# A two-layer hybrid decoder trunk: a joined last product, an enforced order of the wide matmuls, and the weight tiles below the residual tiles

## The chip, the cores and the metric

The kernel runs on one core of one Trainium2 chip. The metric is the device time of one execution in microseconds, the median of several runs. The core has TensorE (matmuls into PSUM), VectorE (DVE in the profile), ScalarE (ACT), GpSimd (POOL), a queue SP that issues most transfers, and 16 DMA engines. SBUF is the working memory on 128 partitions; PSUM has eight banks of 128 x 512 fp32.

## The reference

A causal decoder trunk on 256 tokens of width 2048, in fp32, with two layers. Cut to what matters:

```python
for l in range(2):
    h = rmsnorm(x, norm_mix[l])
    x = x + (even_mixer if l == 0 else odd_mixer)(h, ...)   # in-projection, mixing, out-projection
    h = rmsnorm(x, norm_ffn[l])
    x = x + conv_ffn(h, ffn_w_up[l], ffn_conv_w[l], ffn_w_down[l])
return rmsnorm(x, norm_final)

def conv_ffn(h, w_up, conv_w, w_down):
    g, u = split(h @ w_up)            # 2048 -> 2 x 5632
    g = causal_dwconv(g, conv_w)      # width 3, along the tokens
    return (silu(g) * u) @ w_down     # 5632 -> 2048
```

Layer 0 mixes with a dilated sliding-window attention beside a convolution module; layer 1 with a forgetting attention of 16 heads. Every weight is read once from HBM, about 410 MB in all, and every matmul is to keep nearly full fp32 accuracy.

## The kernel before, in words

**Split operands.** A weight or activation is held as hi + lo, two tiles of a reduced fp32 type that one matmul pass takes: hi is the rounded value, lo the rest. A product takes hi·hi, hi·lo and lo·hi.

**The weight stream.** `stream` (L79) loads 1 MB of weights per transfer into one of three `raw` buffers, and for each half ScalarE makes the hi tile (L95) and VectorE the lo tile (L96), with a raised priority (`AHEAD`). hi and lo have four buffers each in the pool `wp`. A new pair of tiles can be made once TensorE has finished with the pair four before.

**Wide products.** `panel_b` (L100) computes four 128-channel blocks of an output panel over all 256 tokens. The weights stand in the array; the moving operand is the split activation, hi and lo side by side. So for each weight tile there is one matmul of 512 columns with the hi weights (L111, `acc_g`, `acc_u`, `acc_d` and so on by the product's name) and one of 256 columns with the lo weights (L115). A panel over 16 k-tiles has 64 such pairs. The products g and u (up-projection, 22 panels each), d (down-projection of layer 0), q and k of layer 1, `oc` and `ob` (out-projections) run so; the moving operand is `xs` for g, u, q and k, the hidden tile `hp` for d, and `y2` for the out-projections. Layer 0's in-projections use the narrow form (`wide=False`, three matmuls of 256 columns). `panel_a` (L131) is the other way round: the activations stand, 512 weight columns move, three matmuls per k-tile (L127 to L129).

**What sets the order.** The program is traced in order, and a planner then orders each engine's instructions by priority and by the time at which it reckons their inputs ready. Within one engine that order is fixed when the program runs. So the matmuls of a wide product stand in the order the planner gave, which is not everywhere the traced one (hi, lo, hi, lo): where it reckons a lo tile late, it puts several hi matmuls ahead.

**Memory.** Pools are laid out in SBUF in the order in which they are opened: `keep` (constants, the residual stream `xT` and its split form `xs`), then `wp` (raw, hi, lo), then `wk` and what the layers open. In PSUM, `pacc` has five banks for the products' sums and `pms` three for the rest.

**The end.** Layer 1's FFN calls `down1` (L618) twice. The second call handles the last 20 k-tiles of the down-projection in token-major form (`acc_e`). It first closes the scope of both PSUM pools (L629) and opens one pool with eight banks, one for each of four output panels and two token halves. It then goes through the k-tiles four at a time for all panels, and the last four in two steps of two. In the last step all four panels are done for the first token half and then for the second, with `finish_rows` (L660) after each: it adds the residual (L616), sums squares on ScalarE (L664), takes the reciprocal root (`rsqrt_cols`, L154), multiplies by the norm's weights on GpSimd (L669), scales on VectorE and ScalarE (L673, L675), and issues one output transfer a panel (L676).

Of the kernel before, what the change touches and what calls it, by code (L numbers as in the profile page):

```python
# [37 lines left out]
AHEAD, BEHIND, TAIL = 400, 300, 60  # L38
# [3 lines left out]
def trunk(ctx, tc, a):  # L42
    nc = tc.nc
    V, S, PE, G = nc.vector, nc.scalar, nc.tensor, nc.gpsimd

# [53 lines left out]

    def panel_b(src_of, x2, kts, name, order=(0, 1, 2, 3), dk=4, wide=True):  # L100
# [3 lines left out]
        acc = {m: pacc.tile([P, 512], F32, tag="acc", name=f"acc_{name}_{m}") for m in order}  # L104
        for ks, hi, lo in stream(src_of, len(kts), P * len(order), name, dk):
            for m in order:
                ms = slice(m * P, (m + 1) * P)
                for j, k in enumerate(ks):
                    x = x2(kts[k])
                    if wide:  # L110
                        PE.matmul(acc[m], hi[:, j, ms], x.rearrange("p a t -> p (a t)"), start=k == 0, stop=False)  # L111
# [3 lines left out]
                    PE.matmul(acc[m][:, :T], lo[:, j, ms], x[:, 0, :], start=False, stop=k == len(kts) - 1)  # L115
# [38 lines left out]
    def rsqrt_cols(ps, scale, name, n=2):  # L154
# [7 lines left out]
        V.tensor_tensor(out=t, in0=r, in1=r, op=ALU.mult)  # L162
        V.tensor_tensor(out=t, in0=t, in1=v, op=ALU.mult)
# [496 lines left out]
    def finish_rows(acc, t):  # L660
        for i in range(4):
            cs = slice(512 * i, 512 * (i + 1))
            add_o(acc[i][t], t, i)
            S.activation(junk[:, 512 * (i % 2):512 * (i % 2) + 512], o[:, t, cs], AF.Square, accum_out=fs[:, t, i:i + 1])  # L664
        V.reduce_sum(out=sf[:, t:t + 1], in_=fs[:, t, :], axis=AX.X)
        rf = rsqrt_cols(sf[:, t:t + 1], 1.0 / D, f"fin{t}", 1)
        for i in range(4):
# [72 lines left out]
```

## Time and profile before

| | |
|---|---|
| runs | 2240.04, 2237.7, 2239.58 us; median 2239.58 |
| the profiled execution | 2240.73 us; its span 2238.9 us, granted TensorE clock 0.996 |
| TensorE (matmul) | busy 2213.6 us, 99% of the span |
| VectorE, ScalarE, GpSimd | 67%, 50%, 1% |
| HBM read | 409.84 MB, 184 GB/s over the span |

The span runs from the first to the last instruction; the execution's time is 1.8 us longer. Matmuls are pipelined: a row's duration is longer than the distance to the next matmul's start, so rates are read from start to start. In a row of the timeline stand start, duration, engine, source line, operation, output<-inputs, shapes and count, and in brackets the idle time before it and what released it. A row of windows has the stretch, its length, the busy time and count of each engine (TensorE's matmuls, its weight loads, VectorE, ScalarE, GpSimd), the granted clock, the DMA share and GB/s. A row of the groups has the count, then busy us, mean ns, idle before and its releasers.

### The profile page before, as it was taken

To read this page: it belongs to the slowest core of one execution; us is meant where nothing else is said; L and a number is where in the kernel's file an instruction comes from. 1 tells how busy PE (TensorE), PEld (TensorE's weight loads), DVE (VectorE), ACT (ScalarE), POOL (GpSimd) and SP (SyncE) were. 2 spreads that over 40 slices of the span, in tenths; PEclk is the share of its full clock that TensorE was granted. 3 is DMA by queue.
4 is the path that set the end of the run, shared out by engine and by line. 5 is a ranking of instruction groups with operands and counts; after the bars stand their busy time and mean duration, and the time that the engine had idled before them with its cause. 6 is when DMAs were issued, how large, how long until landed. Compare 5 with 4: busy or idle time off the path is not lost.

```text
span 2238.9 us, 31976 instructions
## 1 busy us (share of the span) xinstructions
PE 2213.6 (99%) x12778; PEld 1944.4 (87%) x12778; DVE 1493.3 (67%) x2280; ACT 1120.4 (50%) x1579; POOL 26.0 (1%) x58
## 2 busy tenths in 40 slices
PE   8999999999999999999999999999999999999997
PEld 8999988888888888888888888888888888888886
DVE  6999988767754577666655555677666644676644
ACT  6567665544443445444554554455544433454433
POOL 0000000000000000000000000000000000000001
PEclk9999999999999999999999999999999999999999
DMA  8544445555555555555544444555555555555453
GB/s 289 182 183 169 162 177 188 188 188 189 188 188 188 188 188 189 188 189 188 189 173 170 170 170 170 188 183 193 188 188 188 188 190 195 188 185 188 168 194 122
DMA packets 60806, 414.08 MB, mean 185 GB/s; under 512 B 7296, under 2 KB 8000, under 8 KB 12272
## 3 DMA queue, kind: packets, MB, share of 16 engines
q1 hardware_dynamic: 59904, 410.72, 51.2%
q8 instruction: 100, 1.64, 0.3%
q10 hardware_dynamic: 144, 1.05, 0.1%
q0 software_dynamic: 608, 0.26, 0.0%
q14 instruction: 50, 0.41, 0.0%
HBM read 409.84 MB, written 2.10 MB: 184 GB/s over the span
## 4 chain that ended last, share of the span: by engine, by line
PE 97%; DMA 1%; DVE 1%; ACT 0%; SPq 0%; issue 0%; ACTq 0%; DVEq 0%
PE acc_g L111 15%; PE acc_u L111 14%; PE acc_g L115 7%; PE acc_u L115 7%; PE acc_d L111 7%; PE acc_d L115 4%; PE acc_oc L111 3%; PE acc_k L111 3%; PE acc_q L111 3%; PE acc_q L115 2%; PE acc_k L115 2%; PE acc_d L127 2%; PE acc_d L129 2%; PE acc_v L128 2%; PE acc_v L129 2%; PE acc_v L127 2%
## 5 line engine op out<-in xcount | busy, mean ns | idle before, releaser
L111 PE MATMUL acc_g<-xs,whi_g 128*128 128x512 f32 x1408 | 493.0, 397 | 0.0
L111 PE MATMUL acc_u<-xs,whi_u 128*128 128x512 f32 x1408 | 481.9, 395 | 0.0
L115 PE MATMUL acc_g<-xs,wlo_g 128*128 128x256 f32 x1408 | 388.7, 280 | 0.0
L115 PE MATMUL acc_u<-xs,wlo_u 128*128 128x256 f32 x1408 | 370.0, 279 | 0.0
L96 DVE TENSOR_TENSOR wlo_g<-raw_g,whi_g 128x1024 fp32r<-128x1024 f32 x176 | 215.2, 1224 | 166.3 <-ACT whi_g L95 166.3
L111 PEld LDWEIGHTS acc_g<-xs,whi_g 128*128 128x128 f32 x1408 | 262.6, 188 | 60.5
L111 PEld LDWEIGHTS acc_u<-xs,whi_u 128*128 128x128 f32 x1408 | 260.1, 188 | 52.7
L95 ACT CAST whi_u<-raw_u 128x1024 fp32r<-128x1024 f32 x176 | 185.1, 1052 | 239.6 <-PE acc_u L111 122.0
L96 DVE TENSOR_TENSOR wlo_u<-raw_u,whi_u 128x1024 fp32r<-128x1024 f32 x176 | 213.3, 1222 | 116.2 <-ACT whi_u L95 116.2
L95 ACT CAST whi_g<-raw_g 128x1024 fp32r<-128x1024 f32 x176 | 184.9, 1052 | 198.3 <-PE acc_u L111 93.3
L96 DVE TENSOR_TENSOR wlo_d<-raw_d,whi_d 128x1024 fp32r<-128x1024 f32 x136 | 166.5, 1225 | 161.4 <-ACT whi_d L95 161.2
L115 PEld LDWEIGHTS acc_u<-xs,wlo_u 128*128 128x128 f32 x1408 | 265.0, 188 | 9.0
L115 PEld LDWEIGHTS acc_g<-xs,wlo_g 128*128 128x128 f32 x1408 | 265.6, 189 | 3.0 <-DVE wlo_g L96 0.2
L95 ACT CAST whi_d<-raw_d 128x1024 fp32r<-128x1024 f32 x136 | 143.0, 1051 | 207.2 <-PE acc_d L111 118.8
L111 PE MATMUL acc_d<-hp,whi_d 128*128 128x512 f32 x704 | 245.2, 394 | 0.0
L115 PE MATMUL acc_d<-hp,wlo_d 128*128 128x256 f32 x704 | 194.4, 283 | 0.0
L111 PEld LDWEIGHTS acc_d<-hp,whi_d 128*128 128x128 f32 x704 | 131.3, 188 | 28.8
L115 PEld LDWEIGHTS acc_d<-hp,wlo_d 128*128 128x128 f32 x704 | 132.4, 188 | 1.9
L115 PE MATMUL acc_q<-xs,wlo_q 128*128 128x256 f32 x384 | 106.0, 283 | 0.0
L115 PE MATMUL acc_k<-xs,wlo_k 128*128 128x256 f32 x384 | 105.8, 281 | 0.0
L111 PE MATMUL acc_q<-xs,whi_q 128*128 128x512 f32 x256 | 90.6, 396 | 0.0
L96 DVE TENSOR_TENSOR wlo_e<-raw_e,whi_e 128x1024 fp32r<-128x1024 f32 x40 | 48.9, 1225 | 60.4 <-ACT whi_e L95 60.4
(305 smaller groups left out, 4178.0 us busy)
## 6 DMA issues: line engine op xcount, KB each, us to landing
raw_g<-in_ffn_w_up SPq DMA_DIRECT2D x88, 1024.0 KB, 4.7
raw_u<-in_ffn_w_up SPq DMA_DIRECT2D x88, 1024.0 KB, 4.8
raw_d<-in_ffn_w_down SPq DMA_DIRECT2D x68, 1024.0 KB, 4.7
raw_q<-in_od_w_in SPq DMA_DIRECT2D x16, 1024.0 KB, 4.8
raw_k<-in_od_w_in SPq DMA_DIRECT2D x16, 1024.0 KB, 4.8
raw_v<-in_od_w_in SPq DMA_DIRECT2D x16, 1024.0 KB, 4.7
raw_oc<-in_od_w_out SPq DMA_DIRECT2D x16, 1024.0 KB, 4.8
raw_e<-in_ffn_w_down SPq DMA_DIRECT2D x16, 1024.0 KB, 4.8
```

The costliest lines, as they stand in the source:

```text
L95: S.copy(hi, rv[:, h:h + half, :])
L96: last = V.tensor_tensor(out=lo, in0=rv[:, h:h + half, :], in1=hi.bitcast(F32), op=ALU.subtract)
L111: PE.matmul(acc[m], hi[:, j, ms], x.rearrange("p a t -> p (a t)"), start=k == 0, stop=False)
L115: PE.matmul(acc[m][:, :T], lo[:, j, ms], x[:, 0, :], start=False, stop=k == len(kts) - 1)
L127: PE.matmul(o, xh, hi, start=first, stop=False)
L128: PE.matmul(o, xh, lo, start=False, stop=False)
L129: PE.matmul(o, xl, hi, start=False, stop=last)
```

## The change

It has five parts.

1. The pool `wp` is opened ahead of `keep`, so the weight tiles lie at lower addresses and `xT` and `xs` above them.
2. `in_order` adds, for every matmul of the wide products, a dependency on the one traced before it, with no semaphore: the planner must keep the traced order within and across wide products. Other matmuls can still stand between.
3. The last product keeps the PSUM pools: three of its eight sums take the banks of `pms` and five those of `pacc`.
4. The last four k-tiles of the last product are loaded in four transfers of 1 MB and split into eight pairs of tiles that all stay: two pairs in the tiles of the gate (`gp`, `cv`), one in a spare `hp` tile, four in the normal buffers, one in a `raw` buffer. Then for each token half, and in it for each panel, come 12 matmuls, the residual's add, the squares and, for panels 0 to 2, the multiplication with the norm's weights, now on VectorE. After the four panels come the reciprocal root and the scaling in the order 1, 0, 3, 2, which for panel 3 includes the norm's weights.
5. In `rsqrt_cols`, for one column, two multiplications become one instruction.

```diff
-    keep = ctx.enter_context(tc.tile_pool(name="keep", bufs=1))
     wp = ctx.enter_context(tc.tile_pool(name="wp", bufs=4))
+    keep = ctx.enter_context(tc.tile_pool(name="keep", bufs=1))
...
-                    hi = room.tile([P, half, width], F32R, tag="gp", name=f"whi_{name}_{c + h}", bufs=2)
-                    lo = room.tile([P, half, width], F32R, tag="cv", name=f"wlo_{name}_{c + h}", bufs=2)
+                    hi, lo = room(f"{name}_{c + h}")
...
+    issued = [None]
+
+    def in_order(*args, **kw):
+        i = PE.matmul(*args, **kw).ins
+        if issued[0] is not None:
+            tc.add_manual_dep(i, issued[0].name, mybir.DependencyInfo(mybir.DependencyClass.NoSync, mybir.DependencyReason.DATA),
+                              reason="order of a product's matmuls")
+        issued[0] = i
...
+        mm = in_order if wide else PE.matmul
...
-                        PE.matmul(acc[m], hi[:, j, ms], x.rearrange("p a t -> p (a t)"), start=k == 0, stop=False)
+                        mm(acc[m], hi[:, j, ms], x.rearrange("p a t -> p (a t)"), start=k == 0, stop=False)
...
-        V.tensor_tensor(out=t, in0=r, in1=r, op=ALU.mult)
-        V.tensor_tensor(out=t, in0=t, in1=v, op=ALU.mult)
+        if n == 1:
+            V.scalar_tensor_tensor(out=t, in0=r, scalar=v, in1=r, op0=ALU.mult, op1=ALU.mult)
...
-        ps_scope.close()
-        pl = ctx.enter_context(tc.tile_pool(name="pl", bufs=1, space=bass.MemoryType.PSUM))
-        acc = [[pl.tile([P, 512], F32, name=f"acc_e{i}{t}") for t in range(2)] for i in range(4)]
+        acc = [[None, None] for i in range(4)]
+        for b, (i, t) in enumerate((i, t) for i in range(4) for t in range(2)):
+            acc[i][t] = misc(f"acc_e{i}{t}") if b < 3 else pacc.tile([P, 512], F32, tag="acc", name=f"acc_e{i}{t}")
...
-        for i in range(4):
-            for got in part(i, at, KC):
-                for t in range(2):
-                    rows(i, t, at, *got)
-        at = n - KC
-        last = [next(part(i, at, KC, room=fp if i > 1 else None)) for i in range(4)]
+        rooms = [from_gate] * 2 + [from_hidden] + [from_weights] * 4 + [from_raw]
+        last = [list(part(i, at, 4, room=lambda nm: rooms.pop(0)(nm))) for i in range(4)]
         for t in range(2):
             for i in range(4):
-                rows(i, t, at, *last[i])
-            with tc.high_priority(offset=TAIL * t):
-                finish_rows(acc, t)
+                for got in last[i]:
+                    rows(i, t, at, *got)
+                add_o(acc[i][t], t, i)
+                cs = slice(512 * i, 512 * (i + 1))
+                S.activation(junk[:, 512 * (i % 2):512 * (i % 2) + 512], o[:, t, cs], AF.Square, accum_out=fs[:, t, i:i + 1])
+                if i < 3:
+                    V.tensor_tensor(out=o[:, t, cs], in0=o[:, t, cs], in1=gb[:, cs], op=ALU.mult)
+            V.reduce_sum(out=sf[:, t:t + 1], in_=fs[:, t, :], axis=AX.X)
+            rf = rsqrt_cols(sf[:, t:t + 1], 1.0 / D, f"fin{t}", 1)
+            for i in (1, 0, 3, 2):
+                cs = slice(512 * i, 512 * (i + 1))
+                if i == 3:
+                    V.scalar_tensor_tensor(out=o[:, t, cs], in0=o[:, t, cs], scalar=rf, in1=gb[:, cs], op0=ALU.mult, op1=ALU.mult)
+                elif i == 1:
+                    V.tensor_scalar(out=o[:, t, cs], in0=o[:, t, cs], scalar1=rf, scalar2=None, op0=ALU.mult)
+                else:
+                    S.activation(o[:, t, cs], o[:, t, cs], AF.Copy, scale=rf)
+                nc.sync.dma_start(out=a["out"][t * P:(t + 1) * P, cs], in_=o[:, t, cs])
```

`from_gate`, `from_hidden`, `from_weights` and `from_raw` each return a hi and a lo tile of two k-tiles by 512 columns from the tiles named in part 4; `from_hidden` and `from_raw` cut both out of one larger tile.

More of the change, by code (lines that the diff above doesn't have):

```diff
@@ L37 @@
 ACT_TAPS = (1,)
-AHEAD, BEHIND, TAIL = 400, 300, 60
+AHEAD, BEHIND = 400, 300
 @with_exitstack
@@ L44, in trunk @@
     V, S, PE, G = nc.vector, nc.scalar, nc.tensor, nc.gpsimd
+    wp = ctx.enter_context(tc.tile_pool(name="wp", bufs=4))
     keep = ctx.enter_context(tc.tile_pool(name="keep", bufs=1))
-    wp = ctx.enter_context(tc.tile_pool(name="wp", bufs=4))
     wk = ctx.enter_context(tc.tile_pool(name="wk", bufs=2))
-    ps_scope = ctx.enter_context(ExitStack())
-    pacc = ps_scope.enter_context(tc.tile_pool(name="pacc", bufs=5, space=bass.MemoryType.PSUM))
-    pms = ps_scope.enter_context(tc.tile_pool(name="pms", bufs=3, space=bass.MemoryType.PSUM))
+    pacc = ctx.enter_context(tc.tile_pool(name="pacc", bufs=5, space=bass.MemoryType.PSUM))
+    pms = ctx.enter_context(tc.tile_pool(name="pms", bufs=3, space=bass.MemoryType.PSUM))
     def misc(name):
@@ L110, in panel_b @@
                     if wide:
-                        PE.matmul(acc[m], hi[:, j, ms], x.rearrange("p a t -> p (a t)"), start=k == 0, stop=False)
+                        mm(acc[m], hi[:, j, ms], x.rearrange("p a t -> p (a t)"), start=k == 0, stop=False)
                     else:
-                        PE.matmul(acc[m][:, :T], hi[:, j, ms], x[:, 0, :], start=k == 0, stop=False)
-                        PE.matmul(acc[m][:, :T], hi[:, j, ms], x[:, 1, :], start=False, stop=False)
-                    PE.matmul(acc[m][:, :T], lo[:, j, ms], x[:, 0, :], start=False, stop=k == len(kts) - 1)
+                        mm(acc[m][:, :T], hi[:, j, ms], x[:, 0, :], start=k == 0, stop=False)
+                        mm(acc[m][:, :T], hi[:, j, ms], x[:, 1, :], start=False, stop=False)
+                    mm(acc[m][:, :T], lo[:, j, ms], x[:, 0, :], start=False, stop=k == len(kts) - 1)
         return acc
@@ L161, in rsqrt_cols @@
         t = wk.tile([P, n], F32, tag="rs_t", name=f"t_{name}")
-        V.tensor_tensor(out=t, in0=r, in1=r, op=ALU.mult)
-        V.tensor_tensor(out=t, in0=t, in1=v, op=ALU.mult)
+        if n == 1:
+            V.scalar_tensor_tensor(out=t, in0=r, scalar=v, in1=r, op0=ALU.mult, op1=ALU.mult)
+        else:
+            V.tensor_tensor(out=t, in0=r, in1=r, op=ALU.mult)
+            V.tensor_tensor(out=t, in0=t, in1=v, op=ALU.mult)
         V.tensor_scalar(out=t, in0=t, scalar1=-0.5, scalar2=1.5, op0=ALU.mult, op1=ALU.add)
@@ L646, in down1, with from_gate, from_hidden @@
                         rows(i, t, at, *got)
-        at = n - 4
-        for i in range(4):
-            for got in part(i, at, KC):
-                for t in range(2):
-                    rows(i, t, at, *got)
-        at = n - KC
-        last = [next(part(i, at, KC, room=fp if i > 1 else None)) for i in range(4)]
+        def from_gate(nm):
+            return [fp.tile([P, KC, 512], F32R, tag=tag, name=f"{w}_{nm}", bufs=2) for tag, w in (("gp", "whi"), ("cv", "wlo"))]
+        def from_hidden(nm):
+            both = fp.tile([P, 4, 2, T], F32R, tag="hp", name=f"wboth_{nm}", bufs=6).rearrange("p a b t -> p (a b t)")
+            return [both[:, 1024 * h:1024 * (h + 1)].rearrange("p (k c) -> p k c", k=KC) for h in range(2)]
@@ new lines, in from_weights, with from_raw @@
+        def from_weights(nm):
+            return [wp.tile([P, KC, 512], F32R, tag=w, name=f"{w}_{nm}") for w in ("whi", "wlo")]
+        def from_raw(nm):
+            both = wp.tile([P, 2 * KC * 512], F32, tag="raw", name=f"wboth_{nm}", bufs=3).bitcast(F32R)
+            return [both[:, 1024 * h:1024 * (h + 1)].rearrange("p (k c) -> p k c", k=KC) for h in range(2)]
+        rooms = [from_gate] * 2 + [from_hidden] + [from_weights] * 4 + [from_raw]
+        at = n - 4
+        last = [list(part(i, at, 4, room=lambda nm: rooms.pop(0)(nm))) for i in range(4)]
@@ L654, in down1 @@
         for t in range(2):
             for i in range(4):
-                rows(i, t, at, *last[i])
-            with tc.high_priority(offset=TAIL * t):
-                finish_rows(acc, t)
[L660 to L667, printed above, removed]
-            cs = slice(512 * i, 512 * (i + 1))
-            G.tensor_tensor(out=o[:, t, cs], in0=o[:, t, cs], in1=gb[:, cs], op=ALU.mult)
-        for i in range(4):
-            cs = slice(512 * i, 512 * (i + 1))
-            if i % 2 == 0:
-                V.tensor_scalar(out=o[:, t, cs], in0=o[:, t, cs], scalar1=rf, scalar2=None, op0=ALU.mult)
-            else:
-                S.activation(o[:, t, cs], o[:, t, cs], AF.Copy, scale=rf)
-            nc.sync.dma_start(out=a["out"][t * P:(t + 1) * P, cs], in_=o[:, t, cs])
+                for got in last[i]:
+                    rows(i, t, at, *got)
```

1 line of the change is left out of this document (added).

## The prediction

> **What bounds the kernel now.** I read the page first: engine totals, the chain that ended last, the costliest groups.
>
> ```profile
> span 2238.9 us, 31976 instructions
> ...
> PE 2213.6 (99%) x12778; PEld 1944.4 (87%) x12778; DVE 1493.3 (67%) x2280; ACT 1120.4 (50%) x1579; POOL 26.0 (1%) x58
> ...
> PE 97%; DMA 1%; DVE 1%; ACT 0%; SPq 0%; issue 0%; ACTq 0%; DVEq 0%
> ...
> L111 PE MATMUL acc_g<-xs,whi_g 128*128 128x512 f32 x1408 | 493.0, 397 | 0.0
> L111 PE MATMUL acc_u<-xs,whi_u 128*128 128x512 f32 x1408 | 481.9, 395 | 0.0
> ...
> L96 DVE TENSOR_TENSOR wlo_d<-raw_d,whi_d 128x1024 fp32r<-128x1024 f32 x136 | 166.5, 1225 | 161.4 <-ACT whi_d L95 161.2
> ...
> L111 PE MATMUL acc_d<-hp,whi_d 128*128 128x512 f32 x704 | 245.2, 394 | 0.0
> ```
>
> TensorE is the bound: 97% of the chain. So time can come only from TensorE standing still, running at a lower clock, or spacing its matmuls wider than it must, and from what follows the last matmul. The diff touches all of these: the junction to the last product and the tail after it ("the joined end"), and the spacing of the wide products (order and addresses).
>
> **The junction.** Next, the timeline where the last wide product (acc_u) hands over to the last down product (acc_e), the granted clock there, and two entries of the chain for the steady rate.
>
> ```profile
> 2110.68 0.28 PE L115 MATMUL acc_u<-xs,wlo_u 128*128 128x256 f32 x1
> ...
> 2113.80 0.42 DVE L123 TENSOR_TENSOR half_u<-acc_u,half_u 128x256 f32<-128x256 f32 x1
> ...
> 2114.27 0.79 PE L127 MATMUL acc_e<-whi_e,hp 128*128 128x512 f32 x1 [3.32 <-DVE half_u L123]
> ...
> 2120.27 0.39 PE L129 MATMUL acc_e<-whi_e,hp 128*128 128x512 f32 x1
> ```
>
> ```profile
> 2113.30:2120.00 6.70, 5.73 (x14) 4.47 (x15) 2.35 (x7) 2.05 (x4) 0.00 (x0) 0.50 0.41 157
> 2120.20:2200.00 79.80, 79.80 (x350) 65.46 (x350) 35.53 (x29) 30.48 (x30) 0.00 (x0) 1.00 0.46 165
> ```
>
> ```profile
> 2124.78 0.23 PE acc_e L127
> ...
> 2198.94 0.23 PE acc_e L127
> ```
>
> L629 closes the pools of acc_u before the eight tiles of acc_e are made, so the first acc_e matmul waits until VectorE has read all of acc_u (L123, ending at 2114.22). The change gives the first three tiles banks of the misc pool, the fourth the spare fifth bank of pacc, and the rest acc_u's banks, which are read out by 2114.2 while the first panel alone has 24 matmuls. The first acc_e matmul uses the first hidden block, made long before. So it can start one 256-column step after 2110.68, at 2110.80. The 14 matmuls ahead of the one at 2120.27 then take 14 × 0.229 us (36 steps of nine matmuls between the two chain entries: 74.16 / 324) and that one starts at 2114.01 instead: **6.3 us saved**, of which some 2.8 us is the half clock (0.50 in the window, 14 matmuls at about 0.43). The bounds: if acc_e's first bank still waited for the last read of acc_u, nothing; if only the stall shrank and the clock still fell, 3.5.
>
> The Trainium skill's "TensorE: Matmul & The Clock Gate" (Part 1: The HAM clock gate) says the clock halves after about one idle window of 3.4 us and recovers after a busy one; the trace agrees, with 3.3 us idle and 0.50 until about 2120. By that rule a stall cut to 1 us would already give the clock back whole, so the bound of 3.5 could not occur; the sum is the same.
>
> **The tail.** The timelines of four engines around the last matmuls.
>
> ```profile
> 2217.09 0.39 PE L129 MATMUL acc_e<-whi_e,hp 128*128 128x512 f32 x1
> ...
> 2226.80 0.39 PE L129 MATMUL acc_e<-whi_e,hp 128*128 128x512 f32 x1
> ```
>
> ```profile
> 2217.52 0.69 DVE L616 TENSOR_TENSOR o<-acc_e,o 128x512 f32<-128x512 f32 x1 [1.27 <-PE acc_e L129]
> ...
> 2225.24 1.20 DVE L162 TENSOR_TENSOR t_fin<-r_fin 128x1 f32<-128x1 f32 x1
> 2226.47 1.20 DVE L163 TENSOR_TENSOR t_fin<-t_fin,v_fin 128x1 f32<-128x1 f32 x1
> ...
> 2230.96 0.16 DVE L665 TENSOR_REDUCE sf<-fs 128x1 f32<-128x4 f32 x1 [0.85 <-ACT xT L664]
> ...
> 2231.77 0.51 DVE L162 TENSOR_TENSOR t_fin<-r_fin 128x1 f32<-128x1 f32 x1
> ...
> 2232.51 0.15 DVE L164 TENSOR_SCALAR t_fin<-t_fin 128x1 f32<-128x1 f32 x1
> ```
>
> ```profile
> 2218.78 0.18 ACT L664 ACTIVATION_READ_ACCUMULATOR xT<-o 128x1 f32 x1
> 2232.95 1.33 ACT L675 ACTIVATE o<-o,r_fin 128x512 f32<-128x512 f32 x2 [1.41 <-DVE r_fin L165]
> 2221.35 6.30 POOL L669 TENSOR_TENSOR o<-o,xT 128x512 f32<-128x512 f32 x5 [1.01 <-ACT xT L664]
> ```
>
> The last matmul ends at 2227.19, the last scaling starts at 2232.95: 5.76 us. In it VectorE is late because the first half's finish is mixed into the second's (one-element operations of 1.20 us, while GpSimd multiplies, stand ahead of the second half's add). The change runs the first half of the tokens through all four panels (last four k-tiles) and then the second, so the first half's finish lies under 4 × 12 matmuls (11.0 us) and is over when the second half ends; GpSimd is out; the weighting of panels 0 to 2 moves to VectorE ahead of the last sum, that of panel 3 into the scaling.
>
> Unqueued, the path is: the matmul that ends at 2217.48 is followed by the add at 2217.52 and the accumulator read that ends at 2218.96, so the sum is ready 1.48 us after the matmul; 0.03 us to the reduction (by its twin at 2230.96, after a read that ended at 2230.93). From there to the scaling it takes 1.99 us now; L162 to L164 (0.74) become one operation of about 0.20, so 1.45. In all 2.96 instead of 5.76: **2.8 us saved**. Behind the scaling nothing shrinks: ScalarE scales two panels as now (1.33) and the last output leaves behind them. Bounds: 1.5 (if VectorE's weighting of panel 2, about 0.7 by the L616 row, or the longer scaling of panel 3 gets into the path) and 3.3 (if the eight output issues no longer queue together).
>
> The six weightings that come to VectorE (three panels, two halves, about 0.7 us each) lie under matmuls. The four last loads are split into eight pairs of tiles; three go to tiles free since the last u panel, four to the normal buffers, one to a load buffer.
>
> **The order and the addresses of the wide products.** One (hi 512, lo 256) pair per weight tile; 2816 pairs in g and u, 704 in d, 512 in q and k, 256 in oc, 128 in ob. Two chain entries one g and one u panel apart, and the timeline at the ends of stretches in which hi and lo alternate strictly today:
>
> ```profile
> 473.38 0.92 PE acc_u L111 x4
> ...
> 518.25 0.92 PE acc_u L111 x4
> ```
>
> ```profile
> 1539.41 0.40 PE L111 MATMUL acc_g<-xs,whi_g 128*128 128x512 f32 x1
> ...
> 1551.89 0.40 PE L111 MATMUL acc_u<-xs,whi_u 128*128 128x512 f32 x1
> ...
> 2073.61 0.40 PE L111 MATMUL acc_g<-xs,whi_g 128*128 128x512 f32 x1
> ...
> 2087.74 0.40 PE L111 MATMUL acc_g<-xs,whi_g 128*128 128x512 f32 x1
> ...
> 629.84 0.39 PE L111 MATMUL acc_d<-hp,whi_d 128*128 128x512 f32 x1
> ...
> 654.77 0.40 PE L111 MATMUL acc_d<-hp,whi_d 128*128 128x512 f32 x1
> ...
> 304.44 0.40 PE L111 MATMUL acc_ob<-y,whi_ob 128*128 128x512 f32 x1
> ...
> 317.87 0.40 PE L111 MATMUL acc_ob<-y,whi_ob 128*128 128x512 f32 x1
> ```
>
> The mean is 44.87 us / 128 = 350.5 ns a pair. The stretches give 36 pairs at 346.7, 40 at 353.3, 71 at 351.1 and 38 at 353.4. So the same strict order runs at one of several steady spacings. On xs it is 346.7 wherever nothing has disturbed the order; 353.3 comes in g panels behind a place where the planner issued two hi matmuls in a row, and ends at the next such place. Take those away and g and u should stay at 346.7: 128 × 3.8 ns = 0.49 us for each of 22 panel pairs, less four that run so already (the stretch at 1539): 8.8 us; q and k (512 pairs, at the same excess, 1.9, of which I count half, since part of it is waits for the norm) 1. d, oc and ob keep theirs. **About 10 us saved.** The bounds are the spacings seen: all g, u, q, k at 353.4 is 12 us lost; d, oc and ob falling to 346.7 as well is 5 more saved.
>
> What strictness may cost is a wait for lo. It does not bind:
>
> ```profile
> 2095.52 1.22 DVE L96 TENSOR_TENSOR wlo_u<-raw_u,whi_u 128x1024 fp32r<-128x1024 f32 x1
> ...
> 2099.63 1.08 PE L111 MATMUL acc_u<-xs,whi_u 128*128 128x512 f32 x4
> ```
>
> This is where the planner issues four hi matmuls ahead, the tightest place of a u panel; its lo tile was ready at 2096.74, 2.9 us before. With that cover gone each panel would wait by what is missing.
>
> The swap of pools moves the weights and xs; other tiles stay. The Trainium skill's "SBUF — State Buffer" (SBUF: two separate sides) has TensorE read through ports of its own, two of them, which never wait on anyone, so by it the swap costs and gains nothing, and the sum is 2220.5 with rival 1 out. But 351.1 on hp and 353.4 on y beside 346.7 on xs, in the same order, is a sign that the place of the operands counts; no run here moves them.
>
> **Sum.** Span 2238.9 − 6.3 − 2.8 − 10 = 2219.8; the profiled execution took 2240.73, 1.8 more than its span, so 2221.6. The median of the runs shown, 2239.58, is 1.15 below it: **2220.5 us**.
>
> **The rivals.**
> 1. *Place decides the spacing.* The weights' new place gives xs a spacing like those of hp and y, and g and u stay near their mean of 350.5. For: three operands, three spacings. Against: on xs itself two spacings exist at one place, so history matters. Junction and tail alone: 2239.58 − 9.1 = 2230.5.
> 2. *The order locks in the wide spacing.* Strict from the start and nothing to break it: all wide pairs at 353.4. g and u: 18 panel pairs × 0.37 us + 4 × 0.86 = 10.1; q and k 1.5; d 704 × 2.3 ns = 1.6; oc about 0.8. 2230.5 + 14 = **2244.5, slower than before**. It decides from a mean of about 352.6 on (9.1 us over 4416 pairs is 2.1 ns). For: stretches of 353 last a whole panel. Against: every stretch on xs that follows a fresh start is at 346.7.
> 3. *The end starves.* In the first pass of the end a pair of tiles lasts only six matmuls (1.37 us). If the splits do not run ahead, VectorE has 2 × 1.23 + 0.69 + about 0.7 a panel against 2.75 of TensorE: 1.1 us × 4 panels, so 2220.5 + 4.4 = 2225. Against: three pairs of tiles need no released buffer.
> 4. *More spacings fall:* d, oc and ob go to 346.7 too, 5 us more: 2215.5. Against: d and ob hold theirs through every disturbance.
>
> **How the numbers follow.** Forecast 0.42, rivals 0.32, 0.12, 0.08, 0.06. The range of 8 in 10, 2213 to 2239, holds the forecast, rivals 1, 3 and 4, and small mixtures with 2; it leaves out rival 2 and a spacing below any seen. About 0.2% (4.5 us) is what a measurement of this kernel tells from no change: faster than 2235.1 are all but rival 2 and a mixed part of 1, 0.80; within, 0.12; slower, 0.08.
>
> **What would show it.** Junction: no TensorE gap near the first acc_e matmul and a clock of 1.0 there; if a gap of over 1 us stays, that step is wrong. Tail: about 3.0 us from the last matmul's end to the last scaling. Order: g and u panel pairs 44.4 us apart with no run of two hi matmuls; 44.9 is rival 1, 45.2 rival 2. Rival 3 shows as VectorE-released gaps in the last 22 us. A time outside 2213 to 2239 makes the whole wrong.

## The result: no faster, 0.15% slower

| | before | after |
|---|---|---|
| median of 20 runs each | 2239.40 us (2237.03 to 2242.97) | 2242.68 us (2239.65 to 2245.53) |
| ratio to before | 1 | 1.0015, 95% interval 1.0009 to 1.0022 |
| profiled execution, its span | 2240.73, 2238.9 us | 2240.98, 2239.2 us |
| end of the last matmul | 2227.19 us | 2230.42 us |

The forecast was 2220.5 us, with a range of 2213 to 2239; the median lies above the range, and the kernel moved the other way. The profiled execution of after lies in the lower third of its times and that of before in the upper third, so the two profiles are 0.3 us apart where the medians are 3.3 apart. The page of after, in the lines that answer those shown of before:

```profile
span 2239.2 us, 31945 instructions
...
PE 2220.3 (99%) x12778; PEld 1939.8 (87%) x12778; DVE 1491.3 (67%) x2284; ACT 1117.5 (50%) x1579; POOL 15.6 (1%) x50
...
PE 98%; DMA 1%; ACT 1%; DVE 0%; SPq 0%; issue 0%; ACTq 0%; DVEq 0%
...
L102 PE MATMUL acc_g<-xs,whi_g 128*128 128x512 f32 x1408 | 499.0, 398 | 0.0
L102 PE MATMUL acc_u<-xs,whi_u 128*128 128x512 f32 x1408 | 498.7, 397 | 0.0
```

TensorE has the same 12778 matmuls and is busy 6.7 us longer (2220.3 against 2213.6). VectorE's share of the chain went from 1% to 0%, as the joined end was to bring, and yet the kernel is no faster: the matmuls themselves stand wider. The groups point to the place: a hi matmul of `acc_u` has 397 ns where it had 395. In the changed kernel L102 carries the hi and the lo matmuls alike; the weight tile's name tells them apart.

**The junction.** TensorE's timeline where the last u product hands over to `acc_e`, then the windows with the granted clock:

```profile
2118.55 0.28 PE L102 MATMUL acc_u<-xs,wlo_u 128*128 128x256 f32 x1
2118.66 0.39 PE L136 MATMUL acc_e<-whi_e,hp 128*128 128x512 f32 x1
...
2230.02 0.40 PE L138 MATMUL acc_e<-wboth_e,hp 128*128 128x512 f32 x1
```

```profile
2117.70:2124.40 6.70, 6.70 (x32) 5.50 (x31) 6.70 (x15) 5.11 (x10) 0.00 (x0) 1.00 0.58 203
2124.60:2204.40 79.80, 79.80 (x345) 64.70 (x344) 38.60 (x32) 33.89 (x35) 0.00 (x0) 1.00 0.56 202
```

The first `acc_e` matmul starts 0.11 us after the last matmul of u (before: 3.59), and the clock is 1.00 there (before: 0.50). The second window has 345 matmuls in the same 79.80 us in which before had 350: the spacing in the last product is wider too, about 232.6 ns instead of 229.

**The tail.** VectorE's and ScalarE's timelines behind the last matmul, which ends at 2230.42:

```profile
2222.84 0.16 DVE L177 TENSOR_TENSOR r_fin<-r_fin,t_fin 128x1 f32<-128x1 f32 x1
...
2229.19 0.69 DVE L687 TENSOR_TENSOR o<-o,xT 128x512 f32<-128x512 f32 x1 [0.85 <-ACT xT L685]
2230.45 0.69 DVE L628 TENSOR_TENSOR o<-acc_e,o 128x512 f32<-128x512 f32 x1 [0.57 <-PE acc_e L138]
...
2233.25 0.16 DVE L177 TENSOR_TENSOR r_fin<-r_fin,t_fin 128x1 f32<-128x1 f32 x1
```

```profile
2233.44 1.33 ACT L697 ACTIVATE o<-o,r_fin 128x512 f32<-128x512 f32 x2 [0.86 <-DVE r_fin L177]
```

The first half's reciprocal root is done at 2223.00, 7.4 us before the last matmul ends; panel 2's weighting (2229.19) is done before the last sum arrives; and the scaling starts at 2233.44, 3.02 us after the last matmul's end (before: 5.76). From that end to the end of the span it is 8.79 us now and was 11.74.

**Where it went.** Windows over four stretches that hold one kind of product each: the narrow k product of layer 0's mixer, g and u of layer 0's first and second group of panels, and g and u of layer 1's first group. First before, then after:

```profile
150.00:170.00 20.00, 20.00 (x169) 20.00 (x168) 19.86 (x38) 13.73 (x24) 0.00 (x0) 1.00 0.50 181
380.00:580.00 200.00, 200.00 (x1144) 174.35 (x1143) 140.49 (x208) 98.77 (x134) 0.53 (x5) 1.00 0.52 188
770.00:940.00 170.00, 170.00 (x972) 148.25 (x972) 119.71 (x181) 82.94 (x113) 0.32 (x3) 1.00 0.53 190
1570.00:1730.00 160.00, 160.00 (x919) 139.65 (x918) 108.81 (x159) 77.83 (x107) 0.32 (x3) 1.00 0.52 185
```

```profile
150.00:170.00 20.00, 20.00 (x179) 20.00 (x178) 20.00 (x33) 13.57 (x23) 0.00 (x0) 1.00 0.51 186
380.00:580.00 200.00, 200.00 (x1135) 173.69 (x1134) 137.49 (x204) 96.50 (x132) 0.43 (x4) 1.00 0.53 189
770.00:940.00 170.00, 170.00 (x964) 147.63 (x963) 120.12 (x181) 82.36 (x112) 0.32 (x3) 1.00 0.52 186
1570.00:1730.00 160.00, 160.00 (x908) 138.97 (x907) 108.36 (x159) 76.60 (x104) 0.32 (x3) 1.00 0.53 187
```

These windows serve as a ruler in all that follows. The first count in a row is TensorE's matmuls. It includes about two that hang over the edges, so a (hi, lo) pair of g or u takes 2 × 200 us / (1144 − 2) = 350.3 ns before and 2 × 200 / (1135 − 2) = 353.0 after; from the first to the last start in the stretch it is 350.4 and 353.3. The clock is 1.00 in both and TensorE has no gap. After has 353.3 ns in all three stretches of g and u: neither the 346.7 that the prediction counted on nor the old mean. The narrow products go the other way: 20 us hold 179 matmuls instead of 169, 113.3 ns each instead of 120.0.

The starts of the first g matmul of layer 0 and of layer 1 close the account, before and then after:

```profile
349.12 0.63 PE L111 MATMUL acc_g<-xs,whi_g 128*128 128x512 f32 x2
...
1482.50 0.40 PE L111 MATMUL acc_g<-xs,whi_g 128*128 128x512 f32 x1
```

```profile
340.81 0.39 PE L102 MATMUL acc_g<-xs,whi_g 128*128 128x512 f32 x1
...
1482.84 0.40 PE L102 MATMUL acc_g<-xs,whi_g 128*128 128x512 f32 x1
```

| stretch, by starts of its first and last matmul | after less before, us |
|---|---|
| layer 0's mixer, up to the first g | −8.31 |
| layer 0's FFN and layer 1's mixer, up to layer 1's first g | +8.65 |
| layer 1's FFN, up to the last u matmul (2110.68, 2118.55) | +7.53 |
| last u matmul to the last matmul's end: the junction, less the wider last product | −4.64 |
| tail | −2.95 |
| span | +0.28 |

The junction and the tail gave about what was forecast. The stretches of the wide products, which were to give 10 us, took 16, a part of it in the token-major products that lie among them. The mixer's 8.3 us are two things. Up to the first matmul of `acc_ob` after is 9.9 us ahead, by narrow products that no step had counted; then 1.6 us go in `acc_ob`. There the profiled execution of after ran at half clock for 3.4 us (worth about 1.7 us, an estimate from the clock in the row), behind an idle of 1.42 us; of the fourteen traces only after's and e3's (0.50 from 303.7 us) have this, though all have an idle of 1.37 to 1.42 us at that place:

```profile
293.71 0.50 PE L102 MATMUL acc_ob<-y,whi_ob 128*128 128x512 f32 x1 [1.42 <-DVE y L465]
```

```profile
295.30:298.60 3.30, 3.30 (x12) 2.81 (x11) 2.78 (x7) 2.05 (x6) 0.00 (x0) 0.50 0.15 25
```

### The profile page after: what moved, and what is told of

Its sections match the earlier page's. It is cut to its first block, busy times and chain, and to the rows that moved or that the text cites. A ratio compares the mean times of both kernels' runs of the same rounds, so it can differ in the third digit from the quotient of the medians.

```text
span 2239.2 us, 31945 instructions
## 1 busy us (share of the span) xinstructions
PE 2220.3 (99%) x12778; PEld 1939.8 (87%) x12778; DVE 1491.3 (67%) x2284; ACT 1117.5 (50%) x1579; POOL 15.6 (1%) x50
## 4 chain that ended last, share of the span: by engine, by line
PE 98%; DMA 1%; ACT 1%; DVE 0%; SPq 0%; issue 0%; ACTq 0%; DVEq 0%
PE acc_g L102 22%; PE acc_u L102 22%; PE acc_d L102 11%; PE acc_q L102 4%; PE acc_k L102 4%; PE acc_oc L102 4%; PE acc_ob L102 2%; PE acc_d L138 2%; PE acc_d L136 2%; PE acc_d L137 2%; PE acc_v L137 2%; PE acc_v L136 2%; PE acc_v L138 2%; PE acc_e L138 2%; PE acc_e L137 2%; PE acc_e L136 2%
## 5 line engine op out<-in xcount | busy, mean ns | idle before, releaser
L102 PE MATMUL acc_g<-xs,whi_g 128*128 128x512 f32 x1408 | 499.0, 398 | 0.0
L102 PE MATMUL acc_u<-xs,whi_u 128*128 128x512 f32 x1408 | 498.7, 397 | 0.0
L102 PE MATMUL acc_g<-xs,wlo_g 128*128 128x256 f32 x1408 | 396.2, 281 | 0.0
L102 PE MATMUL acc_u<-xs,wlo_u 128*128 128x256 f32 x1408 | 395.6, 281 | 0.0
L102 PEld LDWEIGHTS acc_g<-xs,whi_g 128*128 128x128 f32 x1408 | 264.7, 188 | 65.6 <-issue 0.6
L102 PEld LDWEIGHTS acc_u<-xs,whi_u 128*128 128x128 f32 x1408 | 264.7, 188 | 65.3
L102 PEld LDWEIGHTS acc_g<-xs,wlo_g 128*128 128x128 f32 x1408 | 264.3, 188 | 0.1
L102 PEld LDWEIGHTS acc_u<-xs,wlo_u 128*128 128x128 f32 x1408 | 264.3, 188 | 0.0
L102 PE MATMUL acc_d<-hp,whi_d 128*128 128x512 f32 x704 | 248.7, 396 | 0.0
L102 PE MATMUL acc_d<-hp,wlo_d 128*128 128x256 f32 x704 | 198.2, 282 | 0.0
L102 PEld LDWEIGHTS acc_d<-hp,whi_d 128*128 128x128 f32 x704 | 132.3, 188 | 32.4 <-issue 1.0
L102 PEld LDWEIGHTS acc_d<-hp,wlo_d 128*128 128x128 f32 x704 | 132.1, 188 | 0.0
L102 PE MATMUL acc_q<-xs,whi_q 128*128 128x512 f32 x256 | 91.5, 398 | 0.0
L102 PE MATMUL acc_k<-xs,whi_k 128*128 128x512 f32 x256 | 90.6, 397 | 0.0
L102 PE MATMUL acc_oc<-y,whi_oc 128*128 128x512 f32 x256 | 89.5, 392 | 0.0
L94 DVE TENSOR_TENSOR wlo_v<-raw_v,whi_v 128x1024 fp32r<-128x1024 f32 x48 | 58.7, 1224 | 46.0 <-ACT whi_v L93 45.4
```

The source lines that it names most:

```text
L94: last = V.tensor_tensor(out=lo, in0=rv[:, h:h + half, :], in1=hi.bitcast(F32), op=ALU.subtract)
L102: i = PE.matmul(*args, **kw).ins
```

## The experiments

Two theories stood against each other after the result. In the expectations, the *place* theory (P) says that the addresses of the weight tiles and of `xs` set the spacing, whatever the order; the *order* theory (O) says that a strict order with nothing to break it falls into the 353 ns spacing and stays there. All twelve kernels compute the whole reference. Each was timed beside the kernel before on the same chip (medians of before 2238.4 to 2239.4), and ratios are to that.

The table has, for each kernel, the distance from `xs` to the weight tiles in bytes of one partition modulo 512 (from the addresses in the compiled programs; experiments 5 to 8 say why 512), and the spacing from the first to the last start in the stretches of the ruler: ns of one narrow matmul, and of one (hi, lo) pair (twice the mean of one matmul where the order is loose: before, e2, e4). Each row is one profiled execution. The fifth stretch is 1915 to 2070, g and u of layer 1's second group.

| kernel | distance | narrow, ns | g, u: 380–580 | 770–940 | 1570–1730 | 1915–2070 | median us | ratio, 95% |
|---|---|---|---|---|---|---|---|---|
| before | 0 | 120.0 | 350.4 | 350.1 | 348.7 | 350.0 | 2239.4 | 1 |
| after | 64 | 113.3 | 353.3 | 353.3 | 353.3 | 353.3 | 2242.68 | 1.0015 (1.0009–1.0022) |
| e1 order only | 0 | 120.0 | 346.7 | 353.3 | 346.7 | 346.7 | 2237.7 | 0.9991 (0.9982–1.0001) |
| e2 place only | 64 | 113.3 | 352.6 | 352.5 | 351.5 | 352.5 | 2244.14 | 1.0025 (1.0015–1.0034) |
| e3 end and order | 0 | 120.0 | 346.7 | 353.3 | 346.7 | 346.7 | 2227.5 | 0.9947 (0.9932–0.9962) |
| e4 end and place | 64 | 117.8 | 352.5 | 352.5 | 351.7 | 352.6 | 2235.89 | 0.9989 (0.9979–0.9998) |
| e5 weights up 64 | 64 | 113.3 | 353.3 | 353.3 | 353.3 | 353.3 | 2237.92 | 0.9992 (0.9983–1.0002) |
| e6 all up 64 | 0 | 120.0 | 346.7 | 353.3 | 346.7 | 346.7 | 2229.11 | 0.9957 (0.9940–0.9973) |
| e7 after, xs up 64 | 0 | 120.0 | 346.7 | 353.3 | 346.7 | 346.7 | 2226.65 | 0.9944 (0.9929–0.9959) |
| e8 weights up 32 | 32 | 118.3 | 353.3 | 353.3 | 353.3 | 353.3 | 2244.1 | 1.0023 (1.0013–1.0032) |
| e9 one hi ahead | 0 | 120.0 | 346.7 | 346.7 | 346.7 | 346.7 | 2224.59 | 0.9937 (0.9921–0.9954) |
| e10 two places of xs | 64, then 0 | 113.3 | 353.3 | 353.3 | 346.7 | 353.3 | 2231.38 | 0.9969 (0.9957–0.9981) |
| e11 hp at distance 0 | 0 | 120.0 | 346.7 | 346.7 | 346.7 | 346.7 | 2223.28 | 0.9933 (0.9918–0.9948) |
| e12 all distances | 64, then 0 | 113.3 | 353.3 | 346.7 | 346.7 | 353.3 | 2231.61 | 0.9966 (0.9954–0.9978) |

### 1 to 4: the change in parts

**e1**, the kernel before with the strict order alone:

```diff
+        mm = in_order if wide else PE.matmul
...
-                        PE.matmul(acc[m], hi[:, j, ms], ...
+                        mm(acc[m], hi[:, j, ms], ...
```

> The kernel before with the enforced order of the wide products alone. Theory P (the weights' new place set the wide spacing of 353.4 ns a pair in the changed kernel, the order did not): at the old place strict order stays at 346.7 ns on xs, so g and u panel pairs come 44.4 us apart and the time is about 2239.4 - 10 = 2229. Theory O (strict order locks into the wide spacing at any place): 353.4 ns on all of g, u, q, k, panel pairs 45.2 us apart, about 2239.4 + 10 = 2249.

The ratio is 0.9991, and the interval just holds 1. Neither number was met: the order alone does not lose, but it gains some 2 us and not 10. Its windows say why:

```profile
380.00:580.00 200.00, 200.00 (x1156) 176.34 (x1155) 141.34 (x210) 100.33 (x135) 0.53 (x5) 1.00 0.54 190
...
770.00:940.00 170.00, 170.00 (x964) 147.34 (x963) 120.09 (x181) 82.49 (x112) 0.32 (x3) 1.00 0.53 186
1570.00:1730.00 160.00, 160.00 (x925) 139.83 (x924) 108.63 (x161) 78.36 (x106) 0.32 (x3) 1.00 0.54 189
```

1156 matmuls in 200 us are 346.7 ns a pair, 964 in 170 us are 353.3, 925 in 160 us 346.7 again. At the old place, then, the strict order runs at 346.7 ns in three groups of panels and at 353.3 through the ten panels of layer 0's second group, with the same instructions in the same order on the same operands. Against before, e1's trace is 2.4, 0.9 and 2.0 us shorter in the three groups, 2.1 us longer in the second one, and 1.5 us longer in `ob`, d and `oc` together.

**e2**, the kernel before with the two pools swapped alone:

```diff
-    keep = ctx.enter_context(tc.tile_pool(name="keep", bufs=1))
     wp = ctx.enter_context(tc.tile_pool(name="wp", bufs=4))
+    keep = ctx.enter_context(tc.tile_pool(name="keep", bufs=1))
```

> The kernel before with the weights' pool opened first, nothing else. Both theories: the narrow products of layer 0 run at about 114 ns a matmul instead of 120, about 10 us saved up to 310 us, and the token-major products about 3.5 ns wider a matmul, about 4.5 us lost. Theory P: g and u at 353 ns a pair although the order is loose, about 10 us lost in the wide products, in all about 2244. Theory O: g and u keep a mean of about 350, in all about 2234.

```profile
150.00:170.00 20.00, 20.00 (x179) 20.00 (x178) 20.00 (x33) 13.71 (x22) 0.00 (x0) 1.00 0.55 203
380.00:580.00 200.00, 200.00 (x1136) 174.07 (x1135) 137.23 (x204) 96.75 (x131) 0.43 (x4) 1.00 0.53 189
```

Slower, 1.0025 (1.0015 to 1.0034). With the planner's loose order untouched, g and u go from 1144 matmuls in 200 us to 1136, and the narrow products from 169 in 20 us to 179. So the swap sets both, and the strict order is not needed for it: that is the place theory.

**e3**, after with the pools in the old order, and **e4**, after with the planner's loose order:

```diff
-    wp = ctx.enter_context(tc.tile_pool(name="wp", bufs=4))
     keep = ctx.enter_context(tc.tile_pool(name="keep", bufs=1))
+    wp = ctx.enter_context(tc.tile_pool(name="wp", bufs=4))
```

```diff
-        mm = in_order if wide else PE.matmul
+        mm = PE.matmul
```

> The changed kernel with the two pools in their old order: joined end and strict order at the old place. Theory P: g and u at 346.7 ns a pair, the end 9 us shorter, about 2220, faster than both kernels. Theory O: g and u at 353.4, 2239.4 - 9 + 10 = 2240.

> The changed kernel without the enforced order: joined end and new place. Theory P: g and u at 353 as in the changed kernel, so about 2242.7, no change against it. Theory O: g and u at a mean of 350, about 2233.

e3 is faster than both kernels: 2227.5 us, 0.9947. Its junction, free of the wider spacing, gives the size of that step:

```profile
2108.78 0.28 PE L102 MATMUL acc_u<-xs,wlo_u 128*128 128x256 f32 x1
2108.90 0.39 PE L136 MATMUL acc_e<-whi_e,hp 128*128 128x512 f32 x1
...
2218.68 0.40 PE L138 MATMUL acc_e<-wboth_e,hp 128*128 128x512 f32 x1
```

From the last u matmul to the start of the last matmul of all it is 109.90 us; before it was 2226.80 − 2110.68 = 116.12. That is 6.2 us saved. The end as a whole (junction and tail) is worth 10.2 us by the medians of e1 and e3, and 8.3 by those of e2 and e4, about the 9.1 of the prediction.

e4 against after gives the price of the strict order at the new place: the ratios are 0.9989 and 1.0015, so about 5.8 us lost by it. The two traces show most of it. In after the four groups of g and u take 2.0 us more in all, d 2.1, `oc` 0.4 and `ob` 2.2, of which some 1.7 is the half clock. In `ob`, d and `oc` the strict order starts each panel late: e3's first weight load of a d panel at 652.42 us comes 0.18 us behind the load before it, with no wait for another engine shown.

The trace of e4 is of one of the three slowest of its ten runs (2239.9 to 2240.2 us; the other seven are 2234.2 to 2237.0). Its narrow products stand at 117.8 ns, where e2 and after, with the same addresses, have 113.3. So the narrow products too have more than one spacing at one distance.

### 5 to 8: which property of the place

The pools' order changes two things, the tiles' own addresses and the distance between them. One matmul's weights are 128 columns of 4 bytes, 512 bytes of each partition, and its moving row is a multiple of that; so within a product all pairs of operands share their distance modulo 512. Before it is 0 for `xs` (both 64 modulo 512), after it is 64. Four kernels move tiles by a small unused tile in `keep`:

```diff
# e5, e3 with 64 bytes between xs and the weights (e8: 32 bytes)
     xs = keep.tile([P, KT, 2, T], F32R, name="xs")
+    pad = keep.tile([P, 16], F32, name="pad")
+    G.memset(pad, 0.0)
# e6, e3 with 64 bytes ahead of all; e7, after with 64 bytes behind the weights
+    pad = keep.tile([P, 16], F32, name="pad")
+    G.memset(pad, 0.0)
     vcol = keep.tile([P, 88], F32, name="vcol")
```

> Joined end and strict order with the pools in the old order (weights above the residual tiles), and 64 unused bytes per partition between xs and the weights, so that the weights lie 64 bytes further on and xs stays. Start addresses modulo 512: weights 128, xs 64, as in the changed kernel (before: both 64). If the alignment of the tiles makes the spacing, it behaves as the changed kernel: strict pairs on xs at 353.4 ns, narrow matmuls at 114, token-major ones at 232, about 2242. If which pool lies below makes it, it behaves as the kernel with the old place: 346.7, 120, 227 to 229, about 2227.5.

> As the run before, but the 64 unused bytes stand ahead of everything, so weights and xs both lie 64 bytes further on (both 128 modulo 512) and their distance is the old one. If the distance between the two operands makes the spacing: 346.7 and 120, about 2227.5. If the weights' own alignment makes it: 353.4 and 114, about 2242.

> The changed kernel with 64 unused bytes between the weights (below) and the residual tiles, so xs moves to 128 modulo 512 and the weights stay at 128. Distance theory: the old distance modulo 512 is back, so 346.7 and 120, about 2227.5. Weights' own alignment: 353.4 and 114 as in the changed kernel, about 2242.

> Joined end and strict order, pools in the old order, 32 unused bytes between xs and the weights: weights 96 modulo 512, xs 64. A third place, a distance of 32. Distance theory: a spacing of its own, neither of the two; weights' own alignment by steps of 64: as the kernel with the old place, 346.7 and 120, about 2227.5.

Windows of the same two stretches, in the order e5, e6, e7, e8:

```profile
150.00:170.00 20.00, 20.00 (x179) 20.00 (x178) 20.00 (x34) 13.07 (x21) 0.00 (x0) 1.00 0.54 188
380.00:580.00 200.00, 200.00 (x1134) 173.60 (x1133) 138.22 (x204) 96.69 (x132) 0.43 (x4) 1.00 0.53 188
```

```profile
150.00:170.00 20.00, 20.00 (x169) 20.00 (x169) 20.00 (x37) 13.31 (x22) 0.00 (x0) 1.00 0.49 179
380.00:580.00 200.00, 200.00 (x1156) 176.46 (x1155) 141.01 (x210) 100.39 (x135) 0.53 (x5) 1.00 0.54 190
```

```profile
150.00:170.00 20.00, 20.00 (x169) 20.00 (x169) 20.00 (x36) 13.17 (x23) 0.00 (x0) 1.00 0.48 169
380.00:580.00 200.00, 200.00 (x1155) 176.47 (x1154) 140.83 (x210) 100.38 (x135) 0.53 (x5) 1.00 0.54 190
```

```profile
150.00:170.00 20.00, 20.00 (x172) 20.00 (x171) 20.00 (x37) 13.33 (x22) 0.00 (x0) 1.00 0.49 179
380.00:580.00 200.00, 200.00 (x1134) 173.80 (x1134) 139.32 (x209) 98.42 (x132) 0.53 (x5) 1.00 0.53 185
```

Sixty-four unused bytes turn e3 into something like after (e5: 179 and 1134, 2237.92 us) and after into something like e3 (e7: 169 and 1155, 2226.65 us, 16 us less than after). The two are not the same size. In e5, of the operands that meet the weight tiles, only `xs` changes its distance, and by the ratios that costs 10 us; in e7 the hidden tiles and `y2` move with `xs`, and the matmuls of the last product, for one, go back from 232.5 to 229.2 ns. With both tiles moved together nothing changes (e6: 169 and 1156). So it is neither which pool lies below nor a tile's own alignment, but the distance: 0 goes with 120 ns in the narrow products and leaves g and u able to run at 346.7; 64 goes with 113.3 (117.8 in e4's trace) and 353.3. At 32 the narrow products gain little (118.3) and g and u run at 353.3 all the same, which makes e8 the worst of both, 1.0023.

### 9: what picks the spacing at distance 0

At distance 0 both spacings occur. The theory here is that a stretch keeps whatever spacing it starts with until the order is disturbed. **e9** disturbs it once: e3, in which, for four k-tiles of the first panel of layer 0's second group, each hi matmul is issued one place earlier (hi, hi, lo, hi, lo, ...).

```diff
+            if name == "g0_6" and ks[0] == 2:
+                pairs = [(m, j, x2(kts[k])) for m in order for j, k in enumerate(ks)]
+                for n in range(len(pairs) + 1):
+                    if n < len(pairs):
+                        ...  # hi of pair n
+                    if n > 0:
+                        ...  # lo of pair n - 1
+                continue
```

> Joined end and strict order at the old place, with one irregularity put in by hand: in the second chunk of the g panel that opens the second group of layer 0, each hi matmul goes one place ahead of the lo matmul before it. In the run without it, the ten panels of that group (640 pairs) enter from the d product at 353.4 ns and keep it to the end. History theory (a spacing is kept until something disturbs the order): the panels behind it run at 346.7, 640 x 6.7 ns = 4.3 us saved, about 2223. If the stage itself sets 353.4: it comes back within a panel, 2227.5.

Window 770 to 940 of e3, and then of e9:

```profile
770.00:940.00 170.00, 170.00 (x964) 147.51 (x963) 119.73 (x180) 82.81 (x113) 0.32 (x3) 1.00 0.53 186
```

```profile
770.00:940.00 170.00, 170.00 (x982) 148.74 (x981) 121.09 (x182) 83.61 (x114) 0.32 (x3) 1.00 0.54 190
```

964 matmuls become 982: the group goes from 353.3 to 346.7 ns, and stays there through all ten panels, though only the first was touched. The change comes at the touched place. Starts of hi matmuls in e9's first panel, ahead of it and behind it:

```profile
752.85 0.40 PE L102 MATMUL acc_g<-xs,whi_g 128*128 128x512 f32 x1
...
753.91 0.63 PE L102 MATMUL acc_g<-xs,whi_g 128*128 128x512 f32 x2
...
757.08 0.39 PE L102 MATMUL acc_g<-xs,whi_g 128*128 128x512 f32 x1
...
773.03 0.39 PE L102 MATMUL acc_g<-xs,whi_g 128*128 128x512 f32 x1
```

Ahead of it 3 pairs take 1.06 us, 353 ns each; behind it 46 pairs take 15.95 us, 346.7 each. Ten panels of 64 pairs at 6.67 ns are 4.3 us; the spans are 5.9 apart, of which 1.4 is e3's half clock in `acc_ob`, and the medians 2.9. The times alone would not show it, since e3's four runs spread from 2223.9 to 2229.7 us; the trace does. So a stretch keeps its spacing, and one issue out of turn can reset it.

### 10 to 12: versions meant to have both gains

**e10** makes `xs` 64 bytes longer, uses it at distance 64 for layer 0's mixer and at 0 from the FFN on. **e11** is e3 with 128 unused bytes ahead of layer 0's hidden tile, whose distance goes from 128 to 0. **e12** joins both and moves layer 1's `y2` by 160 bytes, to distance 0 as well.

```diff
# e10
+    xsb = keep.tile([P, KT * 2 * T + 16], F32R, name="xs")
+    xs = xsb[:, 0:KT * 2 * T].rearrange("p (k a t) -> p k a t", k=KT, a=2)
...
+        xs = xsb[:, 16:].rearrange("p (k a t) -> p k a t", k=KT, a=2)
         ssq = new_ssq("f0")
# e11
         with tc.tile_pool(name=f"ff{l}", bufs=1) as fp:
+            if l == 0:
+                gap = fp.tile([P, 32], F32, name="gap")
+                G.memset(gap, 0.0)
# e12: both, and
+        gap1 = mx.tile([P, 40], F32, name="gap1")
+        G.memset(gap1, 0.0)
         y2 = mx.tile([P, KT, 2, T], F32R, name="y21")
```

> Joined end and strict order, pools in the old order; xs gets 64 bytes more, layer 0's in-projection uses it 64 bytes ahead (distance from the weights 64 modulo 512), everything after it at distance 0. Distance theory: narrow matmuls at 114 ns instead of 120 (1536 x 6 = 9 us, less what waits for the first loads, and 0.3 us lost in layer 0's v), and the wide ones on xs at 346.7 as before: about 2219 to 2221. If the distance does not decide: 2227.5.

> Joined end and strict order at the old place, with 128 unused bytes ahead of layer 0's hidden tiles, so that their distance from the weights is 0 modulo 512 as that of xs is. Distance theory: d goes from 351.4 to 346.7 ns a pair, 704 x 4.7 = 3.3 us, and if the spacing is carried into the next group's g and u (640 pairs at 353.4), 4.3 us more: 2220 to 2224. If the operand (hp) and not its distance decides: 351.4 stays, 2227.5.

> The two runs before together (xs at two places, hp at distance 0), and layer 1's y2 at distance 0 by 160 unused bytes, so oc goes from 352 to 346.7 (1.3 us). Distance theory: the savings add, 2227.5 - 7.5 - 3.3 - 1.3 and perhaps - 4.3, so 2211 to 2216.

Windows of e10, of e11 and of e12:

```profile
150.00:170.00 20.00, 20.00 (x179) 20.00 (x178) 20.00 (x33) 14.08 (x24) 0.00 (x0) 1.00 0.55 202
380.00:580.00 200.00, 200.00 (x1134) 173.70 (x1134) 137.04 (x204) 96.61 (x131) 0.43 (x4) 1.00 0.53 188
...
1570.00:1730.00 160.00, 160.00 (x925) 141.24 (x924) 109.88 (x163) 79.09 (x108) 0.32 (x3) 1.00 0.54 191
```

```profile
770.00:940.00 170.00, 170.00 (x983) 150.12 (x982) 120.85 (x182) 83.97 (x114) 0.32 (x3) 1.00 0.54 191
```

```profile
770.00:940.00 170.00, 170.00 (x982) 148.69 (x981) 120.61 (x181) 83.11 (x112) 0.32 (x3) 1.00 0.53 189
...
1915.00:2070.00 155.00, 155.00 (x879) 134.52 (x878) 106.51 (x158) 74.95 (x102) 0.22 (x2) 1.00 0.52 187
```

e10 has its narrow gain (179 in 20 us; its first g starts at 340.42 us, e3's at 349.85) and gives it back: its g and u of layer 0 run at 353.3 though their distance is 0. Its trace shows where that begins: from 343 us the first g panel stands at 346.7 ns until, at 359.62 us, two matmuls of the norm's broadcast (`bc_f`) come between, and at 353.3 behind them. A disturbance can thus bring in either spacing. e11 has the lowest median of the study, 2223.28 us, 0.9933 (0.9918 to 0.9948), 15 us below before, though not clear of e9's. Its down products in layer 0 mix panels of 346.7 and 353 (means of 351.2 and 350.0 in the two groups; e3 352.2 and 352.5), and the group behind them runs at 346.7 with no disturbance made (983 matmuls in 170 us), although the last d panel ahead of it stands at 353.4. e12 was to add the savings and does not, 2231.61 us: even in its profiled execution, one of its fastest at 2225.01 us, layer 0's first group and layer 1's second (879 in 155 us) have 353.3. Its runs spread from 2224.3 to 2235.5 us, where those of e11 lie within 3.7. That fits stretches which take the one spacing in some runs and the other in others; as there is one trace, that is only argued.

## Why the prediction was wrong

**Junction: right.** 6.3 us forecast, 6.2 measured in e3. In after itself 4.6 are left of it, because the 480 matmuls of the last product stand some 3.4 ns wider at the new place. The other bounds (nothing, or a smaller stall with the half clock) did not occur. The Trainium skill's "TensorE: Matmul & The Clock Gate" (Part 1: The HAM clock gate) agrees here: with no idle the clock stayed whole, 1.00 in the window where it had been 0.50. At `acc_ob` the measurement differs from the page's idle window of 3.4 us: in after and e3 an idle of about 1.4 us was followed by 3.4 us at half clock. So the prediction's inference that a stall cut to 1 us would give the clock back whole was not safe.

**Tail: right.** 2.96 us forecast from the last matmul's end to the last scaling, 3.02 measured; 2.8 us saved forecast, 2.95 measured to the span's end. The weighting of panel 2 ended at 2229.88, ahead of the last add at 2230.45, so the bound of 1.5 was not reached.

**Rival 3, the end starves: no.** TensorE's window from 2117.70 on is busy throughout, and no start in the last product comes more than 0.3 us behind the one before.

**Rival 4, more spacings fall: in part, and it saved nothing.** Within its panels `ob` did fall, from 353.4 ns a pair to about 346.5:

```profile
299.38 0.39 PE L102 MATMUL acc_ob<-y,whi_ob 128*128 128x512 f32 x1
...
308.04 0.39 PE L102 MATMUL acc_ob<-y,whi_ob 128*128 128x512 f32 x1
```

These are 25 pairs in 8.66 us. `oc` fell likewise, from 350.0 (33 pairs in 11.55 us from 1428.53 in before) to 346.7 (18 pairs in 6.24 us from 1419.74 in after), with the loose order of e4 too. d rose: in after most of its panels stand at 353.3. So "d, oc and ob keep theirs" was wrong, but the late panel starts, d and the half clock took more than this gained.

**The failed step: "the swap of pools moves the weights and xs", and g and u "should stay at 346.7".** The prediction read the 346.7 ns of before's strict stretches as a property of the order on `xs`, and priced the swap at nothing, with 8.8 us saved in g and u. In after's trace the four groups of g and u took 2.5, 2.1, 3.3 and 2.2 us more instead, 10.1 in all. The runs show that the 346.7 belongs to the distance of the operands' addresses: e2 changes the place alone and takes g and u to about 352.5, and 64 bytes in e7 take after's 353.3 back to 346.7. The prediction's own remark that "351.1 on hp and 353.4 on y beside 346.7 on xs" is a sign that the place counts was right, and should have had more weight.

The Trainium skill's "SBUF — State Buffer" (SBUF: two separate sides) was the ground on which the swap was free by a page's rule: TensorE's read ports wait for no other engine. No run here contradicts that sentence, since TensorE shows no wait for anyone in the stretches of g and u; what was wrong was to take it to mean that the place costs nothing. The measurement decides: 2242.68 us against 2226.65 for 64 bytes.

**Rival 1 had the mechanism and a wrong price.** It let g and u stay at the mean of 350.5 ns and came to 2230.5 us. At the new place they run at 353.3, which is **rival 2's** spacing, and its 2244.5 us lies 1.8 above the median. Rival 2's cause, a strict order that locks in the 353.3 by itself, is not the main one: e2 has it without the order. But it is not empty either. At distance 0 ten panels do lock at 353.3 (e1, e3, e6, e7), behind the down product and with nothing disturbed in between, so "on xs it is 346.7 wherever nothing has disturbed the order" was too strong. And at the new place the strict order costs 5.8 us against the loose one. This is the second size that failed: of the 10 us that the order was to bring, it brought about 2 at the old place (e1, interval 0 to 4).

**What no step had.** The swap makes the narrow products of layer 0's mixer faster, 120.0 to 113.3 ns, 9.9 us up to the first matmul of `ob`. The prediction had no term for them; without that gain after would have been some 0.6% slower. The same swap makes the token-major products slower (about 229 to 232.6 ns a matmul in the last one).

**The forecast's number** was nearly that of another kernel, which does not make its reasoning right: the end and the order at distance 0, with the ten locked panels freed, takes 2224.59 us (e9) or 2223.28 (e11), 4.1 and 2.8 us above it.

## What to carry to other kernels

Where TensorE bounds a kernel, read the spacing from start to start for every product, and count in a change of memory layout by the distance of the two operands' addresses: here one unused tile of 64 bytes is worth 10 us (e5 against e3) or 16 us (e7 against after) of 2240. A strict order holds a good spacing as firmly as a bad one; so look at what each stretch starts from, and test a single issue out of turn at its head. Savings of this kind do not add up by themselves (e12), so each layout has to be timed whole.

## What the runs showed of the hardware that was not expected

- TensorE's spacing depends on the distance of the weights' and the moving operand's addresses. Modulo 512 bytes: at 0 the narrow matmuls of 256 columns take 120.0 ns, at 64 113.3 (117.8 in one trace of six), at 32 118.3. The strict pairs of 512 and 256 columns take 346.7 or 353.3 ns at 0, and 353.3 at 64 and 32 in all the stretches of the table. The two steps are of one size: 353.3 − 346.7 = 6.7 and 120.0 − 113.3 = 6.7.
- At distance 0 a stretch keeps its spacing for hundreds of pairs (ten panels of 64, from g to u and back), until the order is disturbed; a disturbance can bring in the shorter spacing (e9) or the longer one (e10).
- An idle of 1.4 us was twice followed by 3.4 us at half clock (after, e3), and twelve times, at the same place, it was not.
- What stays open: why the distance matters, what picks the spacing at the start of a stretch, and the true modulus. Other operands give other spacings within their panels, by the addresses of the compiled programs: 351.1 at 128 (d before), 350.0 at 160 (`oc` before), 353.4 at 288 (`ob` before), 346.7 at 224 and 352 (`oc` and `ob` after). The 351.1 is steady and no mixture of the other two; with the same operand at 0 (e11) panels stand at 346.7 or 353. e7's distance is a multiple of 512 and not of 2048. A modulus of 256 was not told apart from 512, and distances other than 0, 32 and 64 were not tried for `xs`.
